# Attention by pairs of heads: transposes of both heads side by side, value tiles by pairs in one bank, weights' low parts on GpSimd

## The chip, the cores and the metric

One core of a Trainium2 chip runs the whole kernel. The metric is the device time of one execution in microseconds (us). The engines, by their names in the profile: PE is TensorE (matmuls, transposes), DVE VectorE, ACT ScalarE, POOL GpSimd, SP SyncE, which issues most DMA transfers. Each engine works through its own queue in order.

## The reference

One layer of a streaming encoder on a sequence of 1024 tokens with 1024 features.

```python
h = rmsnorm(x, norm_mix_g)
u, q, k, v = split(h @ w_in)            # u: 512 columns, q, k, v: 512 each (8 heads of 64)
y_pool = pool_mixer(u, pool_w, pool_b, pool_scale)   # 4 groups of 128 columns: trailing mean over
                                                     # 2/4/8/16 tokens minus the token, a 128x128 map
y_attn = chunk_attention(q, k, v, rel_bias)          # chunks of 64 tokens: own chunk and 8 before it,
                                                     # bias by clipped distance, softmax
x = x + concat(y_pool, y_attn) @ w_out
x = x + (gelu(conv3(h2 @ w_gate)) * (h2 @ w_up)) @ w_down   # h2 = rmsnorm(x), 2816 hidden columns
x = x + gate(x) * (p @ w_ple)                               # a gated input embedding of 256 columns
out = rmsnorm(x)
```

## The kernel before, in words

**Arithmetic.** Matrices are split into two parts of reduced precision (fp32r): a high part, which ScalarE makes by a rounding copy, and a low part, which VectorE makes by subtracting the high part from the source. `split` (L122, L123) does both. A product is three matmuls: high by high, high by low, low by high (`mm3`, L117 to L119). Wherever the text says "low part", it means that subtraction.

**Stages.** First x is loaded and split, and the first q/k block and half of V are projected (to about 54 us). Then comes the attention stage (54 to 280 us), then the output projection with the pooling mixer between its pieces (to 338 us), then the gated MLP and the embedding.

**The attention stage** goes through 28 units: four pairs of heads, and for each the token tiles (0, 1), 2, 3, 4, 5, 6, 7, of 128 tokens each. `unit(u)` does the following in TensorE's order.
- `probs_t` (L407) transposes the previous unit's probabilities into PSUM, banks 2 and 3 (chunk halves), what doesn't fit there into banks 6 and 7 (the far part). `probs_out` queues their evacuation: ScalarE's high part (L426) and VectorE's low part (L427) into PT, one buffer per head.
- `scores` (L383) multiplies q and k of this unit. `softmax` queues the minimum (L351), the exponential (L363), the reciprocal (L365) and the scaling (L361).
- Then TensorE gets some steps of `fill`, the generator over all projections that remain: q/k of pair 1 and 2, the second half of V, q/k of pair 3, and u in the order of the groups 2, 3, 0, 1. They use banks 0 and 1 in turn. A q/k half is evacuated at L263, a V tile at L254 and L255 with `v_outs`, a u half at L560.
- For an odd last tile, `values` (L451, L452) multiplies the transposed probabilities of two tiles by V, into a free one of banks 0 and 1.
- `run_later` emits up to eight steps of the window sums for u's groups 2 and 3 on GpSimd (`pool_out`, L575 to L589).

**The order of ScalarE's and VectorE's queues.** Every piece of such work is handed to `push` with a time within the unit, in us. `flush` sorts what has been pushed by these times and emits it. `now` is the unit's running time, which grows by 0.68 with each fill step, and `at` is the place within the current bank's projection. If a bank is needed whose evacuation is still unsorted (`owed`), `flush` comes early.

**Weights.** The blocks of w_in are loaded in turn into two raw buffers by SP (L171), and `split_later` queues their two high and two low parts (L475, L472). The weights of V's second half come between them by `v_weights`. The list `blocks_` holds the order of the blocks, with None for V. When block 1 is projected, the weights of V's second half are loaded once more and their first half is split once more; no matmul reads that. The raw buffer of this split is the one into which SP then loads blocks 4 and 5 of w_out (`rawo`).

**The output projection.** `out_weights` loads a block of w_out (L611) and splits it (L122, L123). `out_mm(d, h, bank, ...)` multiplies four blocks by the attention's output, 12 matmuls. `mix(g)` splits a group's pooled values (128x1024), multiplies them by its 128x128 map (six matmuls) and splits the result. TensorE's order in this stage is the program's: eight `out_mm` (z = 0 to 7) with mix(2), mix(3), mix(0), mix(1) between them, then the phase that adds the pooled part.

```python
raw = [f(4 * s, 1024) for s in range(2)]
rawo = [f(2 * s, 512) for s in range(4)]
```

Of the kernel before, what the change touches and what calls it, by code (L numbers as in the profile page):

```python
# [82 lines left out]
def trunk(tc, xT, pT, vecs, w_qk0, w_in, w_v, bias, counts, pool_w, w_out, w_up, w_down,  # L83
# [4 lines left out]
    with tc.tile_pool(name="sb", bufs=1) as sb, \  # L88
# [32 lines left out]
        def split(src, hi, lo, pinned=False):  # L121
            both = (act.activation(hi, src, AF.Copy),  # L122
                    dve.tensor_tensor(lo, src, rv(hi), ALU.subtract))  # L123
            if pinned:
                for i in both:
# [202 lines left out]


        for s in range(2):  # L330
            dve.memset(rv(PT[s][:, :, 0, P:2 * P]), 0.0)
            dve.memset(rv(PT[s][:, :, 5, 0:P]), 0.0)

        def load_bias(h):
            b = biasb[h % 3]
# [5 lines left out]
                pool.memset(b[64:128, 0:64], BIG)  # L341
            return turned

        def softmax(todo):

            for i, (x, b, ps, S, s_) in enumerate(todo):
                z = 2 * i / len(todo)

                def least(b=b, ps=ps, S=S, s_=s_):
                    if len(ps.shape) == 3:  # L350
                        dve.tensor_tensor_reduce(  # L351
                            S.rearrange("p (a b) -> p a b", a=2), ps,
                            b.rearrange("p (a b) -> p a b", a=2), 1.0, BIG, ALU.add, ALU.min, s_[:, 0:1])
                    else:
                        dve.tensor_tensor_reduce(S, ps, b, 1.0, BIG, ALU.add, ALU.min, s_[:, 0:1])

# [8 lines left out]
                push(2.95 + 0.55 * z, lambda s_=s_: dve.reciprocal(s_[:, 2:3], s_[:, 1:2]))  # L365
# [27 lines left out]
        def probs_t(u):  # L393

            c, ts = UNITS[u]
            total = key_tiles(u)

            def place(x, m):
                n = total * x + m
                return (2, HD * n) if n < 8 else (6, 384 + HD * (n - 8))  # L400

            todo = []
            for x in range(2):
                for m in range(total):
                    bank, col = place(x, m)
                    for y in range(2):
                        pe.transpose(PS[:, bank + y, col:col + HD], Sb[x][halves[y], m * P:(m + 1) * P],  # L407
                                     ident[halves[y], halves[y]], tile_position=(HD * y, 0))
                m = 0
                for t in ts:  # L410
                    nk = min(t + 1, BANDT)
                    i0 = max(0, t - 4) - (t // 2 * 2 - 4)
                    edge = min(nk, max(0, 8 - total * x - m))
                    parts = [p for p in ((0, edge), (edge, nk)) if p[1] > p[0]]
                    for a, b in parts:
                        bank, col = place(x, m + a)
                        todo.append((x, t % 2 * P, i0 + a, i0 + b, bank, PS[:, bank:bank + 2, col:col + HD * (b - a)]))
                    m += nk
            return todo

        def probs_out(todo):
            n = 0
            for x, q, a, b, bank, ps in todo:
                src = ps.rearrange("p a (k q) -> p a k q", q=HD)
                hi, lo = [PT[x][:, y, a:b, q:q + P].rearrange("p k (a q) -> p a k q", a=2) for y in range(2)]
                push(3.6 if bank > 3 else 0.3 * n, lambda hi=hi, src=src: act.activation(hi, src, AF.Copy))  # L426
                push(4.4 if bank > 3 else 3.55 + 0.05 * n if n else 2.6, lambda lo=lo, src=src, hi=hi: dve.tensor_tensor(lo, src, rv(hi), ALU.subtract))  # L427
                n += bank < 4

        credit, turns = 0.0, []  # L430

        def values(u):
            nonlocal credit
            c_, ts = UNITS[u]
            w = ts[-1] // 2
            if ts[-1] % 2 == 0:
                return
            while c_ >= 2 and len(v_ready) < 2 * w + 2 or u < NU - 1 and at[0] < 1.6:
                next(fill)
                credit -= 1  # L440
                now[0] += STEP
            flush()
            ks = list(range(max(0, 2 * w - 4), 2 * w + 2))
            bank = (bankn[0] + 1) % 2 if u < NU - 1 else 5
            Os = [PS[:, bank, 256 * j:256 * j + 256] for j in range(2)]
            for j in range(2):
                pt = PT[j]
                O = Os[j]
                for n_, k in enumerate(ks):
                    idx = k - (2 * w - 4)  # L450
                    pe.matmul(O, V[:, k, 2 * c_ + j], pt[:, 0, idx], start=n_ == 0, stop=False)  # L451
                    pe.matmul(O, V[:, k, 2 * c_ + j], pt[:, 1, idx], start=False, stop=n_ == len(ks) - 1)  # L452
# [14 lines left out]
        def split_later(ct, parts, soon=False):  # L467

            t = now[0] - 0.3 if soon else max(5.2, now[0] + 0.4)
            for i, (src, hi, lo) in enumerate(parts):  # L470
                def low(src=src, hi=hi, lo=lo, end=i == len(parts) - 1):
                    dve.tensor_tensor(lo, src, rv(hi), ALU.subtract)  # L472
                    if end:
                        there.add(ct)
                push(t + 0.7 * i * (not soon), lambda src=src, hi=hi: act.activation(hi, src, AF.Copy))  # L475
                push(t + (0.25 + 0.02 * i if soon else 0.8 + 0.7 * i), low)
# [41 lines left out]
        def project_v():  # L518
            v_weights(1)
            flush()  # L520
            order = [(t, z) for t in range(NTOK) for z in range(2)]
            order[1:3] = order[2:0:-1]
            order[-3:-1] = order[-2:-4:-1]
            banks = {}
            for t, z in order:
                if z == 0:
                    bankn[0] += 1
                    banks[t] = bankn[0] % 2
                    if banks[t] in owed:
                        flush()  # L530
                ps = PS[:, banks[t], 0:256]
                paired = t in (0, 1, NTOK - 2, NTOK - 1)
                if (t, z) == (NTOK - 2, 1):
                    weights(8 + 3)
                for k in range(4 * z, 4 * z + 4):
                    mm3(ps, XTH[t // 4][:, k, t % 4 * P:(t % 4 + 1) * P],
                        XTL[t // 4][:, k, t % 4 * P:(t % 4 + 1) * P], wv2[z][0][:, k % 4], wv2[z][1][:, k % 4],
                        k == 0, k == KT - 1)
                    if k % 2:
                        at[0] = 0.36 * (k + 1) if not paired else 0.36 * (k - 3) if z and t % 2 else 0.0  # L540
                        yield True
                if z:
                    hi, lo = v_outs(t, 1, ps)
# [110 lines left out]
        def unit(u):  # L654
# [3 lines left out]
            if u < NU:  # L658
                c, ts = UNITS[u]
                for h in range(2 if ts[-1] > 3 else 1):  # L660
                    while not all((c, x, h) in laid for x in range(2)):
                        next(fill)
                        lay_due(u - 1)
                        flush()
            if u:
                probs_out(probs_t(u - 1))
            if u < NU:
                softmax(scores(u))
# [776 lines left out]
```

## Time and profile before

| | us |
|---|---|
| median of 3 runs | 1140.84 (1140.73 to 1143.66) |
| the profiled execution | 1138.46 |
| its span | 1136.7 |
| TensorE busy in it | 1116.6 (98%) |
| VectorE busy | 866.1 (76%) |
| ScalarE busy | 589.0 (52%) |
| GpSimd busy | 144.2 (13%) |

All times in the text are on the clock of this profiled execution, from the start of its span, which is 1.76 us shorter than the execution. A line of a group of instructions gives the line of the kernel, engine, operation, what it writes and reads, the shape and the count; then busy us and the mean ns of one; then the idle time of the engine ahead of it and what ended that. A line of the timeline begins with its start and its length, for xN from the first start to the last end. A line of a window gives its length, then for PE, weight loads, DVE, ACT and POOL the busy us and the instructions, then the granted clock, the DMA share and GB/s.

### The profile page before, as it was taken

To read this page: it belongs to the slowest core of one execution; us is meant where nothing else is said; L and a number is where in the kernel's file an instruction comes from. 1 tells how busy PE (TensorE), PEld (TensorE's weight loads), DVE (VectorE), ACT (ScalarE), POOL (GpSimd) and SP (SyncE) were. 2 spreads that over 40 slices of the span, in tenths; PEclk is the share of its full clock that TensorE was granted. 3 is DMA by queue.
4 is the path that set the end of the run, shared out by engine and by line. 5 is a ranking of instruction groups with operands and counts; after the bars stand their busy time and mean duration, and the time that the engine had idled before them with its cause. 6 is when DMAs were issued, how large, how long until landed. Compare 5 with 4: busy or idle time off the path is not lost.

```text
span 1136.7 us, 16213 instructions
## 1 busy us (share of the span) xinstructions
PE 1116.6 (98%) x5914; PEld 934.5 (82%) x5914; DVE 866.1 (76%) x1508; ACT 589.0 (52%) x1052; POOL 144.2 (13%) x188
## 2 busy tenths in 40 slices
PE   9999998999999999999999999999999999999997
PEld 7988886888788888888888888888888888888887
DVE  8577757688757888887787777878888789986845
ACT  8376667665654554444444444444444445574634
POOL 0000000064002210120112110211030102000000
PEclk9999999999999999999999999999999999999999
DMA  8111120115500154575557655765576555520003
GB/s 280 36 37 43 38 61 1 59 38 174 178 12 17 42 155 147 134 170 151 133 151 161 159 139 150 155 162 144 149 162 163 139 148 124 155 93 19 1 31 118
DMA packets 64879, 125.91 MB, mean 111 GB/s; under 512 B 7328, under 2 KB 8736, under 8 KB 64800
## 3 DMA queue, kind: packets, MB, share of 16 engines
q1 hardware_dynamic: 50688, 99.38, 26.9%
q0 software_dynamic: 13824, 25.17, 13.8%
q8 instruction: 46, 0.75, 0.3%
q10 hardware_dynamic: 288, 0.33, 0.1%
q14 instruction: 33, 0.27, 0.1%
HBM read 110.18 MB, written 14.68 MB: 110 GB/s over the span
## 4 chain that ended last, share of the span: by engine, by line
PE 92%; DVE 3%; ACT 2%; issue 2%; DMA 1%; SPq 0%; POOL 0%; POOLq 0%; DVEq 0%; ACTq 0%
PE PS L117 29%; PE PS L118 28%; PE PS L119 28%; PE PS L383 2%; PE PS L452 2%; PE PS L451 2%; PE PS L407 2%; DVE F L351 1%; ACT R L122 1%; DMA F<-in_w_qk 1%; DVE B L427 0%; ACT F L602 0%; PE PS L751 0%; DVE F L361 0%; DMA F<-in_w_out 0%
## 5 line engine op out<-in xcount | busy, mean ns | idle before, releaser
L117 PE MATMUL PS<-R 128*128 128x512 f32 (+1 forms) x1104 | 425.0, 385 | 3.4 <-DVE F L263 1.7
L118 PE MATMUL PS<-R 128*128 128x512 f32 (+1 forms) x1104 | 421.6, 382 | 0.1
L119 PE MATMUL PS<-R 128*128 128x512 f32 (+1 forms) x1104 | 421.4, 382 | 0.0
L117 PEld LDWEIGHTS PS<-R 128*128 128x128 f32 x1104 | 207.5, 188 | 47.7 <-issue 2.1
L118 PEld LDWEIGHTS PS<-R 128*128 128x128 f32 x1104 | 207.6, 188 | 40.2 <-DVE R L228 1.3
L119 PEld LDWEIGHTS PS<-R 128*128 128x128 f32 x1104 | 207.5, 188 | 40.3
L122 ACT ACTIVATE R<-F 128x512 fp32r<-128x512 f32 (+2 forms) x221 | 138.3, 637 | 176.9 <-PE PS L118 80.7
L123 DVE TENSOR_TENSOR R<-F,R 128x512 fp32r<-128x512 f32 (+2 forms) x221 | 153.1, 704 | 41.0 <-ACT R L122 39.1
L1144 DVE TENSOR_TENSOR F<-F,PS 128x512 f32<-128x512 f32 x140 | 92.6, 681 | 6.5 <-PE PS L119 6.2
L834 DVE TENSOR_TENSOR F<-F 128x512 f32<-128x512 f32 x88 | 60.5, 687 | 45.6 <-DMA F<-in_w_up 44.9
L122 ACT ACTIVATE BQ<-RW 128x512 fp32r<-128x512 f32 x90 | 52.6, 622 | 78.3 <-PE PS L118 74.2
L1087 POOL DMA_DIRECT2D RW<-Yd x56 | 49.5, 884 | 261.9 <-DMA RW<-Yd 199.9
L1087 POOL DMA_DIRECT2D RW<-in_w_down x40 | 35.7, 937 | 230.8 <-DMA RW<-in_w_down 193.2
L123 DVE TENSOR_TENSOR BQ<-RW,BQ 128x512 fp32r<-128x512 f32 x90 | 59.0, 684 | 2.8 <-PE PS L118 2.1
L118 PE MATMUL PS<-BQ 128*128 128x512 f32 x140 | 54.6, 390 | 0.1
L119 PE MATMUL PS<-BQ 128*128 128x512 f32 x140 | 54.5, 389 | 0.0
L117 PE MATMUL PS<-R,BQ 128*128 128x512 f32 x140 | 54.5, 389 | 0.0
L118 PE MATMUL PS<-R,BQ 128*128 128x512 f32 x140 | 54.5, 389 | 0.0
L119 PE MATMUL PS<-R,BQ 128*128 128x512 f32 x140 | 54.5, 389 | 0.0
L117 PE MATMUL PS<-BQ 128*128 128x512 f32 x140 | 54.5, 389 | 0.0
L970 ACT ACTIVATE F<-F,vec 128x1024 f32<-128x1024 f32 (+1 forms) x25 | 28.6, 1143 | 46.8 <-DVE F L945 42.0
L363 ACT ACTIVATE F<-F,small 128x640 f32<-128x640 f32 (+4 forms) x64 | 44.0, 690 | 13.2 <-DVE small L351 11.5
(179 smaller groups left out, 1706.4 us busy)
## 6 DMA issues: line engine op xcount, KB each, us to landing
F<-in_w_up SPq DMA_DIRECT2D x91, 256.0 KB, 3.9
RW<-Yd SPq DMA_DIRECT2D x60, 256.0 KB, 3.7
RW<-Yd POOLq DMA_DIRECT2D x56, 256.0 KB, 4.9
RW<-in_w_down SPq DMA_DIRECT2D x50, 256.0 KB, 2.9
RW<-in_w_down POOLq DMA_DIRECT2D x40, 256.0 KB, 6.1
Yd<-F SPq DMA_DIRECT2D x40, 256.0 KB, 3.4
F<-in_w_in SPq DMA_DIRECT2D x10, 512.0 KB, 3.4
F<-in_xT SPq DMA_DIRECT2D x16, 256.0 KB, 6.1
```

The source lines that it names most:

```text
L117: pe.matmul(ps, ahi, bhi, start=first, stop=False, skip_group_check=more)
L118: pe.matmul(ps, ahi, blo, start=False, stop=False, skip_group_check=more)
L119: pe.matmul(ps, alo, bhi, start=False, stop=last, skip_group_check=more)
L122: both = (act.activation(hi, src, AF.Copy), dve.tensor_tensor(lo, src, rv(hi), ALU.subtract))
L123: dve.tensor_tensor(lo, src, rv(hi), ALU.subtract))
L363: push(1.9 + 0.85 * z, lambda S=S, s_=s_: act.activation(S, S, AF.Exp, bias=s_[:, 0:1], scale=-1.0, accum_out=s_[:, 1:2]))
L383: pe.matmul(PS[:, places[x][y], 0:wide], q[halves[x], t * P:(t + 1) * P], k[halves[x], ki + y * wide:ki + (y + 1) * wide], start=i == 0, s ...
L407: pe.transpose(PS[:, bank + y, col:col + HD], Sb[x][halves[y], m * P:(m + 1) * P], ident[halves[y], halves[y]], tile_position=(HD * y, 0))
L834: return dve.tensor_tensor(rawu[to], rawu[a], rawu[b], op)
L970: act.activation(y, Gb[:, 2 + a:2 + b], AF.Identity, bias=vec[:, C_CB + fi:C_CB + fi + 1], scale=cw(2))
L1087: pool.dma_start(t, src, accum_op=ALU.add)
L1144: dve.tensor_tensor(t, t, PS[:, 4 + d], ALU.subtract if n in (1, 5) else ALU.add)
```

## The change

It touches five places. (1) PT holds one buffer per precision instead of one per head, and both heads' transposes of a key tile stand side by side, so that one evacuation takes both heads: for a unit with five key tiles two pieces (1024 and 256 elements) instead of three. (2) The evacuations' and the softmax's push times are other ones, which depend on whether values follow (`valued`). (3) The second half of V is projected by pairs of tiles, both in one bank, and its evacuation is queued for the pair; q/k and u halves are evacuated at 3.6 or later. (4) The low parts in `split_later` go to GpSimd, but for block 9 and those that are wanted soon. (5) Each mix stands one `out_mm` earlier.

```diff
-        PT = [r(136 + 12 * s, 3072).rearrange("p (x k q) -> p x k q", x=2, k=6) for s in range(2)]
+        PT = [r(136 + 12 * y, 3072).rearrange("p (k x q) -> p k x q", x=2, k=6) for y in range(2)]
...
-                push(2.95 + 0.55 * z, lambda s_=s_: dve.reciprocal(s_[:, 2:3], s_[:, 1:2]))
-                push(3.9 + 0.1 * z if x else 3.0 + 0.55 * z, scaled)
+                push(max(2.95 + 0.01 * z, 1.91 + 0.85 * z) if valued else 2.95 + 0.55 * z, lambda s_=s_: dve.reciprocal(s_[:, 2:3], s_[:, 1:2]))
+                push(3.9 + 0.1 * z if x else 3.0 + (0.01 if valued else 0.55) * z, scaled)
...
             def place(x, m):
-                n = total * x + m
+                n = 2 * m + x
                 return (2, HD * n) if n < 8 else (6, 384 + HD * (n - 8))
...
-        def probs_out(todo):
-            n = 0
-            for x, q, a, b, bank, ps in todo:
-                src = ps.rearrange("p a (k q) -> p a k q", q=HD)
-                hi, lo = [PT[x][:, y, a:b, q:q + P].rearrange("p k (a q) -> p a k q", a=2) for y in range(2)]
-                push(3.6 if bank > 3 else 0.3 * n, lambda hi=hi, src=src: act.activation(hi, src, AF.Copy))
-                push(4.4 if bank > 3 else 3.55 + 0.05 * n if n else 2.6, lambda lo=lo, src=src, hi=hi: dve.tensor_tensor(lo, src, rv(hi), ALU.subtract))
-                n += bank < 4
+        def probs_out(todo, valued):
+            for q, a, b, bank, ps in todo:
+                src = ps.rearrange("p a (n q) -> p n a q", q=HD)
+                hi, lo = [pt[:, a:b, :, q:q + P].rearrange("p k x (a q) -> p (k x) a q", a=2) for pt in PT]
+                far = bank > 3
+                push(3.5 if far else 0.0, lambda hi=hi, src=src: act.activation(hi, src, AF.Copy))
+                push((3.55 if valued else 4.4) if far else 2.5 if valued else 3.7,
+                     lambda lo=lo, src=src, hi=hi: dve.tensor_tensor(lo, src, rv(hi), ALU.subtract))
...
-                    dve.tensor_tensor(lo, src, rv(hi), ALU.subtract)
+                    (dve if soon or ct == 8 + 1 else pool).tensor_tensor(lo, src, rv(hi), ALU.subtract)
...
-            order = [(t, z) for t in range(NTOK) for z in range(2)]
-            order[1:3] = order[2:0:-1]
-            order[-3:-1] = order[-2:-4:-1]
+            for t0 in range(0, NTOK, 2):
+                bankn[0] += 1
+                bank = bankn[0] % 2
+                if bank in owed:
+                    flush()
+                order = [(t, z) for t in (t0, t0 + 1) for z in range(2)]
+                if t0 in (0, NTOK - 2):
+                    order[1:3] = order[2:0:-1]
+                for i, (t, z) in enumerate(order):
+                    ps = PS[:, bank, 256 * (t % 2):256 * (t % 2) + 256]
...
+                            at[0] = 1.44 * i + 0.36 * (k % 4 + 1)
+                            yield True
+                for z in range(2):
+                    t = t0 + z
+                    hi, lo = v_outs(t, 1, PS[:, bank, 256 * z:256 * z + 256])
                     push(now[0], hi)
                     push(now[0] + 0.5, lo)
-                    owed.add(banks[t])
                     v_ready.append(t)
+                owed.add(bank)
...
-                    push(now[0], lambda: qk_out(x, h, ps))
+                    push(max(now[0], 3.6), lambda: qk_out(x, h, ps))
...
-                push(now[0] + 0.2, lambda: dve.tensor_tensor(U[:, g, HIST + h * 512:HIST + (h + 1) * 512], ps,
+                push(max(now[0], 3.6), lambda: dve.tensor_tensor(U[:, g, HIST + h * 512:HIST + (h + 1) * 512], ps,
...
-            if 2 <= z <= 5:
-                mix((2, 3, 0, 1)[z - 2])
+            if 1 <= z <= 4:
+                mix((2, 3, 0, 1)[z - 1])
```

Lines shift with the edit: L472 is L469 after it, L427 L426, L575 L571, L589 L585, L611 L607.

In GpSimd's queue, the low parts of block 1 now stand where the window sums of u's group 2 end and those of group 3 begin (F is the work area, R and B are split data). The rows before:

```order
L575 TENSOR_TENSOR F<-F 128x265
L585 TENSOR_TENSOR F<-F,small 128x8
L588 TENSOR_TENSOR F<-F,small 128x248
L586 TENSOR_TENSOR F<-F 128x8
L589 TENSOR_TENSOR F<-F 128x248
L575 TENSOR_TENSOR F<-F 128x271
L575 TENSOR_TENSOR F<-F 128x269
```

And after the change:

```order
L571 TENSOR_TENSOR F<-F 128x265
L581 TENSOR_TENSOR F<-F,small 128x8
L584 TENSOR_TENSOR F<-F,small 128x248
L582 TENSOR_TENSOR F<-F 128x8
L585 TENSOR_TENSOR F<-F 128x248
L469 TENSOR_TENSOR B<-F,B 128x512
L571 TENSOR_TENSOR F<-F 128x271
L469 TENSOR_TENSOR B<-F,B 128x512
L571 TENSOR_TENSOR F<-F 128x269
```

Two subtractions have come in, at L469; those of block 0 stand in the same way among the first sums of group 2. The end of the same queue's part in the attention stage, after the change, is the last window sum with the two low parts of the V half that nothing reads:

```order
L571 TENSOR_TENSOR F<-F 128x257
L581 TENSOR_TENSOR F<-F,small 128x16
L584 TENSOR_TENSOR F<-F,small 128x240
L582 TENSOR_TENSOR F<-F 128x16
L585 TENSOR_TENSOR F<-F 128x240
L469 TENSOR_TENSOR R<-F,R 128x512 x2
```

The two subtractions (x2) stood in VectorE's queue before, and GpSimd's ended with the last window sum. In SyncE's queue, the loads of V's half and of w_out stand in the same order as before, with the semaphores on which each waits. Before:

```order
L171 DMA F<-in_w_v 128x1024 [waits DMAHW7_49,DMAHW3_49,DVE_49]
L171 DMA F<-in_w_v 128x1024 [waits DMAHW6_49,DMAHW0_49,DVE_49]
L611 DMA F<-in_w_out 128x512 [waits DMAHW0_49]
L611 DMA F<-in_w_out 128x512
L773 DMA F<-in_xT 128x1024 [waits PE_49,Activation_49,Pool_49]
L773 DMA F<-in_xT 128x1024 [waits DMAHW4_49,PE_49]
L611 DMA F<-in_w_out 128x512 [waits DMAHW7_49,DMAHW5_49,DVE_49]
L611 DMA F<-in_w_out 128x512 [waits DVE_49]
```

And after:

```order
L171 DMA F<-in_w_v 128x1024 [waits DMAHW7_49,DMAHW3_49,Pool_49]
L171 DMA F<-in_w_v 128x1024 [waits DMAHW6_49,DMAHW0_49,Pool_49]
L607 DMA F<-in_w_out 128x512 [waits DMAHW0_49]
L607 DMA F<-in_w_out 128x512
L770 DMA F<-in_xT 128x1024 [waits PE_49,Activation_49]
L770 DMA F<-in_xT 128x1024 [waits DMAHW4_49,PE_49]
L607 DMA F<-in_w_out 128x512 [waits DMAHW7_49,DMAHW5_49,Pool_49]
L607 DMA F<-in_w_out 128x512 [waits Pool_49]
```

The loads have kept their places; four of the waits on VectorE are waits on GpSimd now. The third and fourth load of w_out are its blocks 4 and 5.

More of the change, by code (lines that the diff above doesn't have):

```diff
@@ L330, in trunk @@
         for s in range(2):
-            dve.memset(rv(PT[s][:, :, 0, P:2 * P]), 0.0)
-            dve.memset(rv(PT[s][:, :, 5, 0:P]), 0.0)
+            dve.memset(rv(PT[s][:, 0, :, P:2 * P]), 0.0)
+            dve.memset(rv(PT[s][:, 5, :, 0:P]), 0.0)
         def load_bias(h):
@@ L342, in load_bias, with softmax @@
             return turned
-        def softmax(todo):
+        def softmax(todo, valued):
             for i, (x, b, ps, S, s_) in enumerate(todo):
@@ L398, in place @@
             def place(x, m):
-                n = total * x + m
+                n = 2 * m + x
                 return (2, HD * n) if n < 8 else (6, 384 + HD * (n - 8))
-            todo = []
             for x in range(2):
@@ L408, in probs_t @@
                                      ident[halves[y], halves[y]], tile_position=(HD * y, 0))
[L409 to L418, printed above, removed]
-            return todo
-        def probs_out(todo):
-            n = 0
-            for x, q, a, b, bank, ps in todo:
-                src = ps.rearrange("p a (k q) -> p a k q", q=HD)
-                hi, lo = [PT[x][:, y, a:b, q:q + P].rearrange("p k (a q) -> p a k q", a=2) for y in range(2)]
-                push(3.6 if bank > 3 else 0.3 * n, lambda hi=hi, src=src: act.activation(hi, src, AF.Copy))
-                push(4.4 if bank > 3 else 3.55 + 0.05 * n if n else 2.6, lambda lo=lo, src=src, hi=hi: dve.tensor_tensor(lo, src, rv(hi), ALU.subtract))
-                n += bank < 4
+            todo, m = [], 0
+            for t in ts:
+                nk = min(t + 1, BANDT)
+                i0 = max(0, t - 4) - (t // 2 * 2 - 4)
+                for a, b in ((0, min(nk, 4)), (4, nk)):
+                    if b > a:
+                        bank, col = place(0, m + a)
+                        todo.append((t % 2 * P, i0 + a, i0 + b, bank, PS[:, bank:bank + 2, col:col + 2 * HD * (b - a)]))
+                m += nk
+            return todo
+        def probs_out(todo, valued):
[6 more added lines that the diff above has]
+                     lambda lo=lo, src=src, hi=hi: dve.tensor_tensor(lo, src, rv(hi), ALU.subtract))
         credit, turns = 0.0, []
@@ L446, in values @@
             for j in range(2):
-                pt = PT[j]
                 O = Os[j]
@@ L450, in values @@
                     idx = k - (2 * w - 4)
-                    pe.matmul(O, V[:, k, 2 * c_ + j], pt[:, 0, idx], start=n_ == 0, stop=False)
-                    pe.matmul(O, V[:, k, 2 * c_ + j], pt[:, 1, idx], start=False, stop=n_ == len(ks) - 1)
+                    pe.matmul(O, V[:, k, 2 * c_ + j], PT[0][:, idx, j], start=n_ == 0, stop=False)
+                    pe.matmul(O, V[:, k, 2 * c_ + j], PT[1][:, idx, j], start=False, stop=n_ == len(ks) - 1)
             for j in range(2):
@@ L520, in project_v @@
             flush()
-            order = [(t, z) for t in range(NTOK) for z in range(2)]
-            order[1:3] = order[2:0:-1]
-            order[-3:-1] = order[-2:-4:-1]
[L524 to L543, printed above, removed]
+            for t0 in range(0, NTOK, 2):
[8 more added lines that the diff above has]
+                    ps = PS[:, bank, 256 * (t % 2):256 * (t % 2) + 256]
+                    if (t0, i) == (NTOK - 2, 2):
+                        weights(8 + 3)
+                    for k in range(4 * z, 4 * z + 4):
+                        mm3(ps, XTH[t // 4][:, k, t % 4 * P:(t % 4 + 1) * P],
+                            XTL[t // 4][:, k, t % 4 * P:(t % 4 + 1) * P], wv2[z][0][:, k % 4], wv2[z][1][:, k % 4],
+                            i == 0 and k == 0, k == KT - 1, True)
+                        if k % 2:
+                            at[0] = 1.44 * i + 0.36 * (k % 4 + 1)
[3 more added lines that the diff above has]
+                    hi, lo = v_outs(t, 1, PS[:, bank, 256 * z:256 * z + 256])
@@ L664, in unit @@
                         flush()
+            valued = u > 0 and UNITS[u - 1][1][-1] % 2 == 1
             if u:
-                probs_out(probs_t(u - 1))
+                probs_out(probs_t(u - 1), valued)
             if u < NU:
-                softmax(scores(u))
+                softmax(scores(u), valued)
                 if u % PER == PER - 1:
```

## The prediction

> **What bounds the kernel now.** I read the page first: how busy each engine is, and which engine carries the chain that ended last.
>
> ```profile
> PE 1116.6 (98%) x5914; PEld 934.5 (82%) x5914; DVE 866.1 (76%) x1508; ACT 589.0 (52%) x1052; POOL 144.2 (13%) x188
> PE 92%; DVE 3%; ACT 2%; issue 2%; DMA 1%; SPq 0%; POOL 0%; POOLq 0%; DVEq 0%; ACTq 0%
> ```
>
> TensorE is the bound. The change takes no matmul away, so it can gain only what TensorE waits for, and lose by new waits. Work taken off VectorE and ScalarE counts only there. Next I read what ends TensorE's waits in the stretch where the second half of V is projected (127 to 181 us), and TensorE's busy time there.
>
> ```profile
> PE PS L407 <- DVE B L427: 2.0, 2, 1.8
> PE PS L452 <- DVE B L427: 2.0, 1, 2.0
> PE PS L117 <- DVE F L263: 1.7, 1, 1.7
> PE PS L117 <- DVE R L255: 1.2, 1, 1.2
> PE PS L451 <- ACT B L426: 0.8, 1, 0.8
> 127.00:137.00 10.00, 8.19 (x96) 7.48 (x97) 6.92 (x16) 6.08 (x13) 0.00 (x0) 1.00 0.17 52
> 147.00:157.00 10.00, 9.79 (x116) 9.24 (x117) 7.93 (x24) 9.02 (x23) 0.29 (x2) 1.00 0.24 68
> 157.00:167.00 10.00, 8.81 (x65) 8.23 (x64) 5.96 (x16) 5.04 (x12) 0.00 (x0) 1.00 0.19 54
> 167.00:180.00 13.00, 8.42 (x88) 6.92 (x88) 7.38 (x24) 9.31 (x23) 0.29 (x2) 1.00 0.12 40
> ```
>
> The waits add up to 7.7 us, and the idle time of the four windows to 1.81 + 0.21 + 1.19 + 4.58 = 7.8. All of them are late evacuations: of transposed probabilities (L426/L427), a V bank (L255), a q/k bank (L263). The change rearranges these.
>
> The second place is what surrounds the last projection and the output projection: GpSimd, the loads of w_out, and VectorE's queue behind them.
>
> ```profile
> 240.00:250.00 10.00, 10.00 (x70) 8.10 (x69) 8.51 (x22) 7.56 (x16) 9.06 (x16) 1.00 0.16 52
> 250.00:260.00 10.00, 9.70 (x85) 8.22 (x85) 8.66 (x18) 5.22 (x12) 9.26 (x13) 1.00 0.32 105
> 260.00:270.00 10.00, 10.00 (x73) 8.78 (x69) 5.82 (x10) 4.80 (x10) 9.37 (x15) 1.00 0.54 160
> 269.72 1.15 POOL L589 TENSOR_TENSOR F<-F 128x240 f32<-128x240 f32 x1
> 264.11 0.88 DVE L472 TENSOR_TENSOR R<-F,R 128x512 fp32r<-128x512 f32 x1 [0.79 <-ACT R L475]
> 265.02 5.01 SPq L611 DMA_DIRECT2D F<-in_w_out  x3
> F<-in_w_out SPq DMA_DIRECT2D x16, 256.0 KB, 2.8
> 267.92 1.67 ACT L122 ACTIVATE R<-F 128x512 fp32r<-128x512 f32 x3 [1.12 <-DMA F<-in_w_out]
> 268.59 4.63 DVE L123 TENSOR_TENSOR R<-F,R 128x512 fp32r<-128x512 f32 x6 [0.91 <-ACT R L122]
> 302.11 1.23 DVE L123 TENSOR_TENSOR B<-F,B 128x1024 fp32r<-128x1024 f32 x1 [0.17 <-ACT B L122]
> 268.50:280.00 11.50, 11.50 (x58) 9.72 (x57) 10.85 (x15) 6.28 (x11) 2.37 (x4) 1.00 0.69 239
> 280.00:303.40 23.40, 21.03 (x93) 16.87 (x91) 22.18 (x46) 16.92 (x28) 0.00 (x0) 1.00 0.59 179
> 303.39 0.50 PE L118 MATMUL PS<-B 128*128 128x512 f32 x1 [0.77 <-DVE B L123]
> 305.33 0.39 PE L118 MATMUL PS<-R 128*128 128x512 f32 x1
> 310.36 0.39 PE L119 MATMUL PS<-R 128*128 128x512 f32 x1
> ```
>
> Column five of the windows is GpSimd: with its window sums it is busy 27.7 of the 30 us from 240 to 270, and done at 270.87. SyncE issues the load of w_out's block 4 at 265.02, right behind the first half (264.11) of a second split of V's first weights, which nothing reads but whose raw buffer the load takes over. The block lands after 2.8, ScalarE rounds it, and its low part is the first of the row at 268.59. From there VectorE is busy 10.85 + 22.18 = 33.0 of 34.8 us until the low part of mix(1) ends at 303.34 and releases the matmul at 303.39. So the mixes wait for a VectorE queue that starts with block 4. After that two out_mm (24 matmuls, 305.00 to 310.36 and one interval of (310.36 - 305.33)/22 = 0.229) lead to the pooled phase at 310.59.
>
> **The change part by part.** *Pairs of V tiles in one bank, transposes side by side, the new push times.* Prices of the evacuations, from the groups by form of 127 to 181 us:
>
> ```profile
> L427 DVE TENSOR_TENSOR B<-PS,B 128x640 fp32r<-128x640 f32 x4 | 3.3, 818 | 0.0
> L427 DVE TENSOR_TENSOR B<-PS,B 128x384 fp32r<-128x384 f32 x6 | 3.3, 543 | 0.0
> L427 DVE TENSOR_TENSOR B<-PS,B 128x256 fp32r<-128x256 f32 x6 | 2.5, 411 | 0.0
> L255 DVE SCALAR_TENSOR_TENSOR R<-PS,small,R 128x256 fp32r<-128x256 f32 x8 | 3.9, 482 | 4.6 <-ACT R L254 4.6
> L254 ACT ACTIVATE R<-PS,small 128x256 fp32r<-128x256 f32 x8 | 3.7, 464 | 2.7 <-PE PS L119 2.7
> ```
>
> The low parts of a full unit cost VectorE 818 + 543 + 411 = 1.77 us in three pieces. By their slope, (818 - 411)/384 = 1.06 ns an element, the new two (1024 and 256 elements) cost 1.23 + 0.41 = 1.64. What matters is where they stand: ahead of values, the near low part now follows the softmax's first scaling and both follow no V low part. The 32 pieces fewer on each engine are otherwise worth nothing, since TensorE seldom waits for either elsewhere.
> - V and q/k banks (1.2 + 1.7): a bank is now filled by two tiles before the next is needed, twice the time for an evacuation. I take both waits as gone; but four evacuations then come at once (2 x 0.464 and 2 x 0.482), and following the new rows through those units leaves about 0.6 before one set of values.
> - Transposes (2.0): they wait until the preceding near piece is out of its banks. I leave 0.7, where a V pair stands ahead of it.
> - Values (2.0 + 0.8): the far low part now comes right behind the near one. I leave 0.5.
>
> So 7.8 - 1.8 = 6.0: **-6.0 us**. Ends: all gone, -7.8; a pair's evacuation falling just where a low part fell, -3. No row shows a read from PSUM that alternates between two banks every 64 elements. Below nothing has no reason, since the elements are the same. At most a quarter more (411 for 256 elements by L427 against 482 by L255), 0.3 us on the near piece, lies within that end.
>
> Where no values follow, the near low part stands behind all scaling (3.7). It is one piece of up to 1024, so ScalarE's high part, ahead of it, ends later by 384 elements, about 0.4 us by the same slope. Two late units have few projection steps to cover that: 2 x 0.4 = **+0.8**, between 0 and 1.5.
>
> *The low parts on GpSimd.* Of eighteen lows, those of blocks 5, 10, 6, 7, 2, 3 and of V's first half find GpSimd idle (its first window sum starts at 234.39) and are read a projection later. At twice their time they cost nothing. If a projection began sooner, it would wait about 1.3 us.
>
> ```profile
> 234.39 2.19 POOL L575 TENSOR_TENSOR F<-F 128x271 f32<-128x271 f32 x3 [23.79 <-DVE small L365]
> L899 POOL TENSOR_TENSOR F<-TB x4: 1284/1294/1737, 340.4 to 376.7; 128x512 f32<-128x512 f32 x4
> L909 POOL TENSOR_TENSOR TB<-TB 128x512 f32<-128x512 f32 x4 | 8.0, 1996 | 28.9 <-DVE TB L903 18.9 <-DVE R L123 10.0
> 250.25 3.99 POOL L575 TENSOR_TENSOR F<-F 128x271 f32<-128x271 f32 x4
> 250.15 1.74 DVE L472 TENSOR_TENSOR B<-F,B 128x512 fp32r<-128x512 f32 x2
> 261.00 2.16 POOL L575 TENSOR_TENSOR F<-F 128x269 f32<-128x269 f32 x3
> ```
>
> The other six stand among and behind the window sums: two of block 0, two of block 1, then both of the V half that nothing reads. GpSimd is full there, so what is put in shifts its end. A GpSimd operation on 128x512 takes 1.29 (L899). Up to the first unread low there are five: 270.87 + 5 x 1.29 = 277.3. Block 0's low also waits for its high part (its raw data came at least that late before: up to +1.7). Against that, VectorE's L472 pairs no longer slow the sums: four operations took 3.99 beside such a pair where three took 2.16 later, 1.1 us a pair, two pairs, 2.3 in all. So 276.7. **SyncE now waits for GpSimd there**, and every load of w_out behind block 4 waits in SyncE's queue: 276.7 instead of 265.02, +11.7. The way from the issue to the low part (landing 2.8 and rounding, 268.59 - 265.02 = 3.6) is as before, so block 4's low part starts about 280.3 instead of 268.59: **+11.7**.
>
> VectorE's queue is in order, so u's evacuations and mix(2) and mix(3) lie behind that row. Three 512 lows (2.49 us for four of them, so 0.6 each) now stand behind mix(1): -1.8. Of the queue's idle time, 34.8 - 33.0 = 1.7, I let all go. *One out_mm fewer between the mixes:* behind mix(1) stand three instead of two, 12 more matmuls of 0.229: +2.7. The sum is 11.7 - 1.8 - 1.7 + 2.7 = **+10.9** for the start of the pooled phase. The 3.1 us that TensorE waits in the mixes before (300.15 to 304.43) is inside it, since the chain runs over VectorE. Ends: +8.5, if GpSimd gains another 2.3 from a quieter VectorE; +14, if each of the five lows takes L909's 2.0 instead of 1.29.
>
> ```profile
> 302.13 0.49 PE L117 MATMUL PS<-B 128*128 128x512 f32 x1 [1.60 <-ACT B L122]
> ```
>
> Sum: -6.0 + 0.8 + 10.9 = **+5.7 us**. The profiled execution took 1138.46 (span 1136.7 and 1.76 around it), so 1144.2; the median of the runs is 2.4 above it, so **1146.5 us**. 0.3% (3.4 us) is about what a measurement of this kernel can tell from no change.
>
> **The rivals.**
> 1. *GpSimd is done in time (faster).* Without VectorE's lows its sums run at 0.65 (261.00: 2.16 for three) instead of about 1.0, and the unread low ends by 265. Then the w_out chain starts no later than before: -6.0 + 0.8 - 1.8 - 1.7 + 2.7 = -6.0, about 1135. The point from which it decides is 271: a low that ends there makes the output term as large as the V term's gain. Against it: 27.7 of 30 us busy, with five more of 1.29. Chance 0.12.
> 2. *The two cancel.* Block 4 is late by 7 only, so the output term is 10.9 - 4.7 = +6.2, and all of the V waits go (-7.8): with the +0.8 that is -0.8, about 1140. For it: both are ends that I hold possible. Chance 0.20.
> 3. *GpSimd and VectorE hold each other up.* The row at 250.25 shows that a sum of 0.65 takes up to 1.1 beside VectorE's subtraction, and that the pair of subtractions takes 1.74 instead of 1.38. If each of the five lows waits for one such subtraction (0.69), it takes 2.0 as L909's do, block 4 is 3.5 later still: +9.2, 1150. The Trainium skill, page "SBUF — State Buffer", section "SBUF: two separate sides", has it as a rule: a GpSimd operation and a VectorE operation with two SBUF inputs share a port pair that whoever starts first keeps for the whole instruction, and the other blocks. The trace agrees in that row. Chance 0.18.
> 4. *Pairs don't do what they say.* The V waits only move to the values: -2 instead of -6, +9.7, 1150.5. For it: VectorE has 5.96 to 7.93 us of work in 10 there, so a late evacuation is an order, not a load. Chance 0.08.
>
> **How the numbers follow.** My forecast has 0.42; with rivals 3 and 4 slower has 0.68, same 0.20, faster 0.12. The range takes rival 2 with some 2 us below it, and above my sum at its bad ends, -3 + 1.5 + 13 = +11.5: 1138 to 1152.5.
>
> **What would show it.** After the change SyncE's load of w_out's block 4 waits for GpSimd and goes out right behind its first subtraction after the last window sum; VectorE stands idle ahead of block 4's low part; TensorE has new gaps in the first out_mm's block 4 to 7 and ahead of mix(2) and mix(1). The gaps of the V stretch shrink from 7.8 to about 2. I am wrong if GpSimd's last window sum ends no later against TensorE, or if that load does not wait for it, or if TensorE finds other matmuls for the time.

## The result and the profile after

The changed kernel takes 1139.83 us (median of 12 runs, 1138.78 to 1142.72), the kernel before in the same runs 1140.49 (1137.27 to 1143.66): a ratio of the means of 1.0002, interval 0.9990 to 1.0014. Forecast were 1146.5 and slower. The time lies in the range, but there is no difference that can be measured: of the cases it came out as the second rival, in which gain and loss cancel, though not by that rival's terms (see below).

The page of the changed kernel, its engines and its chain:

```profile
PE 1120.2 (98%) x5914; PEld 936.5 (82%) x5914; DVE 848.5 (74%) x1456; ACT 587.2 (51%) x1020; POOL 165.3 (14%) x208
PE 84%; DVE 5%; issue 4%; POOL 3%; DMA 2%; ACT 1%; POOLq 0%; DVEq 0%; ACTq 0%
```

VectorE has 18 us less to do and GpSimd 21 more, and GpSimd, which was not on the chain, now holds 3% of it. TensorE's waits in the whole kernel, the longest groups:

```profile
PE PS L117 <- ACT F L598: 2.3, 2, 1.6
PE PS L117 <- ACT F L918: 2.0, 2, 1.4
PE PS L117 <- ACT B L122: 1.9, 1, 1.9
PE PS L119 <- DVE R L123: 1.7, 1, 1.7
PE PS L406 <- DVE B L426: 1.6, 3, 0.9
```

Nothing of the V stretch is left at the top. Its windows show the same (third field: TensorE's busy us; the stretch is shorter now and ends at about 175):

```profile
127.00:137.00 10.00, 9.86 (x116) 9.17 (x115) 6.93 (x15) 6.57 (x12) 0.00 (x0) 1.00 0.15 54
147.00:157.00 10.00, 10.00 (x103) 9.73 (x103) 7.83 (x27) 9.26 (x24) 0.29 (x2) 1.00 0.24 67
157.00:167.00 10.00, 9.64 (x97) 9.00 (x96) 5.39 (x15) 6.08 (x14) 0.00 (x0) 1.00 0.05 6
167.00:175.00 8.00, 7.68 (x71) 6.27 (x68) 5.34 (x13) 6.85 (x14) 2.20 (x4) 1.00 0.16 61
```

Of the 7.8 us of idle time there, 1.2 are left with the window from 137 (0.35, not shown). The first matmul of the output projection, in the timeline of before:

```profile
279.97 0.39 PE L117 MATMUL PS<-R 128*128 128x512 f32 x1
```

and in that of the changed kernel, with the first of the pooled phase (before: 310.59):

```profile
274.22 0.39 PE L117 MATMUL PS<-R 128*128 128x512 f32 x1
...
312.96 0.39 PE L117 MATMUL PS<-R 128*128 128x512 f32 x1
```

So up to the output projection 5.75 us are won, and within it 38.74 - 30.62 = 8.1 are lost. How, the timelines of GpSimd, SyncE, VectorE and TensorE after the change show:

```profile
266.19 0.70 POOL L585 TENSOR_TENSOR F<-F 128x240 f32<-128x240 f32 x1
266.85 2.53 POOL L469 TENSOR_TENSOR R<-F,R 128x512 fp32r<-128x512 f32 x2
268.16 5.18 SPq L607 DMA_DIRECT2D F<-in_w_out  x4
271.48 3.70 DVE L123 TENSOR_TENSOR R<-F,R 128x512 fp32r<-128x512 f32 x6 [10.15 <-ACT R L122]
277.33 0.50 PE L119 MATMUL PS<-R 128*128 128x512 f32 x1 [1.67 <-DVE R L123]
300.64 1.22 DVE L123 TENSOR_TENSOR B<-F,B 128x1024 fp32r<-128x1024 f32 x1
301.92 0.69 PE L118 MATMUL PS<-B 128*128 128x512 f32 x1 [0.76 <-DVE B L123]
```

The chain is the one forecast: the last window sum, the first unread low part (266.85 to about 268.1), block 4's load at 268.16, VectorE idle for 10.15 us and then full until mix(1)'s low part ends at 301.86. Block 4's low part starts 2.74 us ahead of the output projection, before it was 11.38 ahead: 8.6 us later, where 11.7 were forecast.

One more thing stands in the windows, in the column behind GpSimd's, the granted clock of TensorE:

```profile
278.10:281.50 3.40, 3.40 (x10) 2.62 (x9) 3.37 (x5) 1.15 (x2) 0.00 (x0) 0.51 0.87 277
302.00:305.40 3.40, 3.40 (x9) 2.64 (x9) 1.67 (x3) 2.72 (x5) 0.00 (x0) 0.51 0.83 272
```

Twice TensorE ran at half its clock for 3.4 us, so that its matmuls there took 1.7 us longer each time. The chain that ended last runs over VectorE beside the first of these stretches and over TensorE through the second, so by this profile only the second lengthened the stage. The profiled execution of before has none until 1130 us.

### The profile page after: what moved, and what is told of

Read it like the earlier page. It is cut to its first block, busy times and chain, and to the rows that moved or that the text cites. A ratio compares the mean times of both kernels' runs of the same rounds, so it can differ in the third digit from the quotient of the medians.

```text
span 1140.7 us, 16154 instructions
## 1 busy us (share of the span) xinstructions
PE 1120.2 (98%) x5914; PEld 936.5 (82%) x5914; DVE 848.5 (74%) x1456; ACT 587.2 (51%) x1020; POOL 165.3 (14%) x208
## 4 chain that ended last, share of the span: by engine, by line
PE 84%; DVE 5%; issue 4%; POOL 3%; DMA 2%; ACT 1%; POOLq 0%; DVEq 0%; ACTq 0%
PE PS L117 26%; PE PS L118 26%; PE PS L119 26%; POOL F L571 2%; PE PS L383 1%; DVE R L123 1%; PE PS L406 1%; PE PS L448 1%; PE PS L449 1%; DMA F<-in_w_up 1%; DMA F<-in_w_out 1%; DVE B L123 0%; POOL F L584 0%; DVE B L426 0%; POOL F L585 0%
## 5 line engine op out<-in xcount | busy, mean ns | idle before, releaser
L1084 POOL DMA_DIRECT2D RW<-Yd x56 | 49.2, 879 | 267.4 <-DMA RW<-Yd 201.6
```

Source lines behind the costliest of these rows:

```text
L1084: pool.dma_start(t, src, accum_op=ALU.add)
```

## The experiments

Times are medians, ratios are to the kernel before on the same chip, with their intervals. Where the text gives the start of the pooled phase, it is read from that run's trace.

**Without the unread half of V** (1). The second load and half split, which no matmul reads, are left out of the changed kernel.

```diff
-                    if (h, k) == (0, 2):
+                    if (h, k) == (0, 2) and ct != blocks_[-1]:
                         weights(behind)
```

> The changed kernel without the second load and half split of V's weights, which nothing reads. Theory A (the load of w_out's block 4 waits for GpSimd's unread low part at the end of its queue, and VectorE's queue and the mixes wait for that block): the load goes out before 262 us, VectorE's queue from block 4 to mix(1)'s low part ends by 294 instead of 301.9, the pooled phase starts about 7 us earlier than in the changed kernel, 1132 to 1134 us. Theory B (the loss comes from the mixes' new place and VectorE's queue itself, not from the load): 1138 to 1140 us, as the changed kernel.

1136.01 us, 0.9954 (0.9941 to 0.9967). By the ratios that is 5.5 us less than the changed kernel, where 6 to 8 were expected. Block 4 is loaded long before 262, but mix(2) still starts late, as ScalarE's timeline shows:

```profile
270.66 1.06 ACT L122 ACTIVATE B<-F 128x1024 fp32r<-128x1024 f32 x1 [9.36 <-POOL F L585]
```

It waits for GpSimd's last window sum, which I had left out, and the pooled phase starts at 309.05, 3.9 us earlier than in the changed kernel, where 7 were expected. The mixes have two conditions, w_out's block 4 and the sums themselves, and GpSimd's queue sets both.

**All low parts on VectorE** (2).

```diff
-                    (dve if soon or ct == 8 + 1 else pool).tensor_tensor(lo, src, rv(hi), ALU.subtract)
+                    dve.tensor_tensor(lo, src, rv(hi), ALU.subtract)
```

> The changed kernel with all low parts of split_later back on VectorE. Theory A: block 4 goes out right behind VectorE's unread low part, about 259 us, the attention stage keeps its gain of 5.8 us, so 1134 to 1136 us. Theory B: the queue and the mixes' place are as in the changed kernel, so 1138 to 1140 us.

1134.48 us, 0.9941 (0.9929 to 0.9953): theory A. The pooled phase starts at 303.88 instead of 312.96.

**The kernel before without the unread half** (3), by the same edit as in (1).

> The kernel before without the second load and half split of V's weights, which nothing reads. Theory A: block 4 is loaded some us earlier, the mixes' waits (3.1 us) go in part: 1137 to 1139 us. Theory B: no change, 1140 us.

1140.58 us, 0.9993 (0.9985 to 1.0002): no gain that can be measured. Block 4 was not what held the mixes as long as VectorE did the low parts; theory A was too generous here.

**The kernel before with the low parts on GpSimd** (4), the edit of (2) the other way round.

> The kernel before with only the low parts moved to GpSimd as in the change. Theory A: block 4 waits for GpSimd's unread low part, about 9 us later than before, without any gain in the attention stage: the pooled phase starts 5 to 8 us later, 1146 to 1149 us. Theory B: within 1 us of before.

1147.46 us, 1.0053 (1.0041 to 1.0065). The timelines of GpSimd, SyncE and VectorE:

```profile
273.72 2.54 POOL L472 TENSOR_TENSOR R<-F,R 128x512 fp32r<-128x512 f32 x2
275.03 5.07 SPq L611 DMA_DIRECT2D F<-in_w_out  x4
278.21 4.30 DVE L123 TENSOR_TENSOR R<-F,R 128x512 fp32r<-128x512 f32 x7 [10.66 <-ACT R L122]
```

The load goes out 10.0 us later than before (265.02), and the time follows by 6.0. In this trace the pooled phase starts at 320.01, 9.4 us later than before, above the 5 to 8 expected; three stretches of 3.41 us at half the clock lie ahead of it, in the trace of before there is none. Taken with (2), the sum closes within the intervals: everything but the low parts is worth 0.9941 - 1 = -6.7 us, the low parts alone +6.0, and both together were measured as +0.2.

**Only the pairs of V tiles** (5): the kernel before with the change's `project_v`.

> The kernel before with only the change's V projection (two tiles in one bank). Theory C (V pairs and the transposes' new order each take away part of the 7.8 us of waits between 127 and 181 us): the waits for V's and the q/k bank (2.9 us) go, those of transposes and values stay, 1137 to 1138.5 us. Theory D (one of the two parts does it all): 1134 to 1136 us, or no change.

1135.23 us, 0.9949 (0.9937 to 0.9961): theory D's first case. The V stretch has two waits left:

```profile
PE PS L452 <- DVE B L427: 1.8, 1, 1.8
PE PS L451 <- DVE R L255: 0.4, 1, 0.4
```

The waits for transposes (2.0) are gone too, though the transposes were as before. This trace doesn't show that the pairs took them away: TensorE ran at half its clock from 168.4 to 171.8, which gives the evacuations beside and behind it 1.7 us more. Its output projection starts at 275.59, 4.4 us earlier than before, with that stretch inside.

**Only the transposes side by side and the new push times** (6): the changed kernel with the old `project_v`, the low parts on VectorE and the mixes at their old place.

> The kernel before with only the transposes side by side and the new times in the queue (places 1 and 2, and the q/k and u evacuations at 3.6). Theory C: the waits of transposes and values (4.8 us) go in part, 1136.5 to 1138.5 us. Theory D: 1134 to 1136 us, or no change.

1145.31 us, 1.0038 (1.0022 to 1.0053), slower; neither theory had that. The waits in the V stretch:

```profile
PE PS L406 <- DVE B L426: 2.8, 2, 2.2
PE PS L117 <- DVE F L263: 2.4, 1, 2.4
PE PS L449 <- DVE B L426: 1.6, 1, 1.6
PE PS L448 <- ACT B L424: 0.8, 1, 0.8
PE PS L117 <- DVE R L255: 0.7, 2, 0.3
```

They add up to 8.3 instead of 7.7. The wait for a q/k bank is longer (L263: 2.4 instead of 1.7), which fits its evacuation put off to 3.6 with one tile in a bank, and so are the waits for transposes (2.8 instead of 2.0), which fits the near low part as one piece. That is 0.6 us of the 4.3. The trace holds two more pieces: from 225 us to the output projection TensorE is idle for 1.8 us instead of 0.8, and from 306.5 it runs at half its clock for 3.41 us. The runs went from 1142.3, the profiled one, to 1148.5, and what makes the rest was not settled.

**The mixes at their old place** (7): as (2), with each mix one out_mm later.

```diff
-            if 1 <= z <= 4:
-                mix((2, 3, 0, 1)[z - 1])
+            if 2 <= z <= 5:
+                mix((2, 3, 0, 1)[z - 2])
```

> The changed kernel with the low parts on VectorE and each mix one out_mm later, as before the change. Theory E (the mixes' chain ends no earlier for standing earlier, and the third out_mm behind mix(1) is the price): the 2.4 us that TensorE waits in the mixes go, 1131.5 to 1133.5 us. Rival (the earlier mixes are a gain of their own): 1135 to 1137 us.

1133.83 us, 0.9939 (0.9927 to 0.9951). The place of the mixes is worth nothing that can be measured beside (2): mix(1)'s low part ends 4 us later (298.4 instead of 294.4) with one out_mm fewer behind it, and the pooled phase starts at 305.7 instead of 303.9; the medians don't show that. The time lies between the two theories, and the waits did not go: TensorE waits 2.8 us in the mixes, 2.0 in (2). The ratio against (5) shows what the transposes and their times add once V goes by pairs: 1.4 us in the medians, within both intervals.

**The waits filled with matmuls** (8): 24 further matmuls, whose results nothing reads, in the changed kernel.

```diff
+        fill_up(8, 7)
         for z, d in enumerate(first_d):
             out_mm(d, 0, first_b[z], attn, True, False)
             if 1 <= z <= 4:
+                if z in (2, 4):
+                    fill_up({2: 7, 4: 9}[z], 1)
                 mix((2, 3, 0, 1)[z - 1])
```

> The changed kernel with 24 further matmuls whose results nothing reads, 8 ahead of the first out_mm, 7 ahead of mix(3), 9 ahead of mix(1), where TensorE waits anyway. Theory F (a window of 3.41 us in which TensorE works little is followed by 3.41 us at half its clock, 1.7 us each time): no such stretch between 270 and 310 us, the granted clock there is 1.00, and 1137 to 1138.5 us although there is more work. Rival (the clock falls for another reason): 1139.5 to 1141 us.

1142.20 us, 1.0011 (1.0003 to 1.0020), a miss, and no clean one: the scheduler places ScalarE's work anew behind the added matmuls, and mix(3) now waits longer for mix(2)'s evacuation. The waits, and TensorE's window behind them:

```profile
PE PS L117 <- ACT F L598: 3.4, 1, 3.4
...
290.00:295.00 5.00, 3.49 (x8) 2.84 (x9) 4.96 (x12) 4.84 (x8) 0.00 (x0) 0.52 0.65 197
```

Behind the filled places ahead of the first out_mm and of mix(1) the clock stays at 1.00. The new wait, ahead of mix(3), which the seven matmuls there don't fill, has 6.83 us at half the clock behind it, from 290.2 on. That speaks for theory F, but it tells nothing of the price.

**Only the twelve early low parts on GpSimd** (9): blocks 0 and 1 and the unread half (the second split of a block that is `in there` already) go back to VectorE.

```diff
-                    (dve if soon or ct == 8 + 1 else pool).tensor_tensor(lo, src, rv(hi), ALU.subtract)
+                    (dve if soon or ct in (8 + 1, 0, 1) or ct in there else pool).tensor_tensor(lo, src, rv(hi), ALU.subtract)
```

> The changed kernel with the low parts of blocks 0 and 1 and of the unread half of V on VectorE, the other twelve on GpSimd. Theory A (the twelve early low parts cost nothing on GpSimd, the six late ones cost it all): as with all of them on VectorE, 1133.5 to 1135.5 us. Rival (each low part on GpSimd costs a share of the 6 us): 1137 to 1139 us.

1132.80 us, 0.9932 (0.9915 to 0.9948), the fastest kernel of the study, 0.7 us below theory A's range and by the ratios 8 us below the changed one. The early ones cost nothing; whether they gain against (2) stays within the intervals. Mix(2) starts in time:

```profile
265.86 1.06 ACT L122 ACTIVATE B<-F 128x1024 fp32r<-128x1024 f32 x1 [1.91 <-POOL F L585]
```

**Only the unread half back on VectorE** (10): the same edit without `0, 1`.

> The changed kernel with only the two low parts of the unread half of V on VectorE. Theory A, as the run without that half refined it (what blocks 0 and 1 put into GpSimd's queue still delays the window sums, and mix(2) waits for the last of them, but block 4 no longer does): 1135 to 1137 us, block 4 loaded by 260 us. Rival (blocks 0 and 1 alone make the loss): 1139 to 1140 us.

1137.38 us, 0.9974 (0.9963 to 0.9985), as refined behind (1), at the upper end. Block 4 is loaded at 260.28 and ready; mix(2) is not:

```profile
263.50 6.00 DVE L123 TENSOR_TENSOR R<-F,R 128x512 fp32r<-128x512 f32 x6 [0.61 <-ACT R L122]
270.82 1.06 ACT L122 ACTIVATE B<-F 128x1024 fp32r<-128x1024 f32 x1 [6.31 <-POOL F L585]
```

Four low parts in GpSimd's queue put off the last sum from 265.8 to 270.8 (5.2 us by four times 1.29), and VectorE's subtractions of w_out, six in 6.00 us instead of 3.70 alone, meet the sums still to be done. By the ratios blocks 0 and 1 cost 4.8 us ((10) against (9)) and the unread half 3.2 (the changed kernel against (10)).

**The parts that paid, together** (11): as (7), without the unread half.

> The changed kernel with the low parts on VectorE, each mix one out_mm later, and without the unread half of V: the parts that paid, together. If block 4's way is what holds the mixes, TensorE's last waits there (3 us) go in part: 1131 to 1133 us. If the window sums hold them, 1133.5 to 1134.5 us, as without that.

1134.99 us, 0.9949 (0.9934 to 0.9964): the window sums hold the mixes; ScalarE waits 6.3 us for the last of them before it splits mix(2). Without the unread half, VectorE's subtractions of w_out start at 258.5 and run beside the last sums, which end at 267.4 instead of 265.8 in (7). Leaving out work that nothing reads gained nothing here.

**Matmuls of one column** (12): 48 of them ahead of the first out_mm of (9), with no engine to wait for.

```diff
+        for _ in range(48):
+            pe.matmul(PS[:, 7, 0:1], ident, ones, start=True, stop=True)
```

> The run with twelve early low parts on GpSimd, with 48 further matmuls of one column (about 0.11 us each, 5.4 us) ahead of the first out_mm, whose results nothing reads; the order of ScalarE's and VectorE's work behind them shifts with that, so its time is not compared, only the granted clock. Theory F (the clock halves behind a window of 3.41 us in which TensorE streams little, whatever it waits for): a stretch of 3.41 us at half the clock begins within 274 to 284 us, where that run had none. Rival (only waits for other engines do it, busy narrow matmuls don't): 1.00 there.

Theory F, by the windows:

```profile
270.00:275.00 5.00, 5.00 (x27) 4.22 (x25) 4.97 (x7) 2.02 (x4) 0.00 (x0) 1.00 0.87 283
280.00:285.00 5.00, 5.00 (x25) 5.00 (x25) 3.97 (x11) 1.35 (x3) 0.00 (x0) 0.50 0.68 218
285.00:290.00 5.00, 5.00 (x25) 5.00 (x25) 0.10 (x1) 0.00 (x0) 0.00 (x0) 0.50 0.20 52
```

By the profile TensorE is busy in every us and waits for nothing, yet at 279.5 the clock falls to half and stays there for 13.65 us, four times 3.41, until wide matmuls have run again. (The 48 show as 96, with up to 0.35 us each at the low clock, so this took longer than planned; its time, 1149.5 in one run, is not compared. They multiply plain fp32 data, the kernel's wide matmuls fp32r, and this run alone doesn't tell width from format.)

## Why the prediction was wrong, point by point

- *The V stretch, -6.0, and the late units, +0.8.* Forecast -5.2, measured -5.75 up to the output projection. Right in sum, wrong in its parts: I gave the V and q/k banks 2.9 us and the transposes and values 4.8. By the ratio of (5) the pairs of V tiles do it nearly alone; by (6) the rest alone is a loss. So the parts are not independent, and a row that names who is late doesn't name who made it late. Why the waits for transposes went was not settled: in the trace of before the longest of them ends at 179.61, and VectorE's last evacuation of V ahead of it starts at 165.18, so V's evacuations did not make that one late.
- *The low parts on GpSimd: the step that failed.* The mechanism was right: by (2), (4), (9) and (10) the whole loss comes from the six late low parts, by the load of block 4 and, which I had missed, by the window sums that the mixes themselves need. The size was wrong, 11.7 against 8.6. I had block 0's low part wait up to 1.7 us for its high part; it did not. And I gave GpSimd back 2.3 us for VectorE's absent subtractions; its sums took 32.2 instead of 36.5 us (229.12 to 266.89 less four low parts of 5.6 in all, against 234.39 to 270.87), so 4.3. These two make 3.7 us, and the way from the load to the low part was 0.25 shorter; against that, the five low parts took 6.9 us instead of 6.45, and the first sum stood 5.3 us earlier instead of 5.75. In (1) and (10), where block 4 came in time and VectorE did w_out's subtractions beside the sums, the same sums took 35.2 us. So about 3 of the 4.3 us came from the delay itself: while the load waited, VectorE had nothing to do that slows the sums. My term had left that out.
- *VectorE's queue and the mixes' place, -1.8 - 1.7 + 2.7 = -0.8.* From block 4's low part to the pooled phase it took 41.5 us instead of 42.0, of which 1.7 are the slow clock from 302.0 on: -2.2 without that. By (7) the earlier mixes are neither a gain nor a loss.
- *The sum.* With the measured terms, -5.75 + 8.6 - 2.2 = +0.7 us instead of +5.7: below what can be told from no change. The miss of 5.0 is 3.1 for GpSimd, 1.4 for the queue and 0.5 for the V stretch.
- *The base.* I set the profiled execution of before 2.4 us below the median and carried that over as a constant. It is not one. In 18 runs of the kernel before beside (5) to (8), the mean clock went from 0.998 (1138.43 us) to 0.993 (1143.03 us): the slow stretches differ from run to run. The pair of profiled executions alone would have said 1142.72 - 1138.46 = +4.3, near the forecast: 1.7 of it are the slow stretch on the chain, of which that of before had none, and 1.6 the longer rest of the program (see the end of this section). Such a pair must not be taken for the result.
- *Rival 1* (GpSimd done in time) fell. *Rival 2* (the two cancel) gave the outcome, but not by its terms: it had block 4 late by 7 and the V term with the late units at -7.0, measured were 8.6 and -5.75, and VectorE's queue made up for it. That the time lies in the range is in part luck. *Rival 3* (the two engines holding each other up) had the price of a low part too high: in the changed kernel three of the four among the sums took 1.29 and one 1.74. The row of (10) shows the effect on VectorE instead, 6.00 against 3.70. *Rival 4* fell with (5).

What stays open: from the start of the pooled phase on, the changed kernel's profile is 1.6 us longer than before's (827.7 against 826.1), with 2.0 us of waits on L918. In the other runs' profiles this rest of the program, which no edit touches, took between 824.8 and 828.1 us; I don't know what sets it.

## What to carry to other kernels

Before moving work to an idle engine, see which of its hours are idle: twelve operations were free on GpSimd while it had nothing else, and six beside and behind its own work cost all that the rest of the change won. Follow every consumer at the end of that engine's queue, a load that takes over a buffer as well as the results that were queued there before. And price a change from several executions where the clock varies; one profile without a slow stretch is a lucky base.

## What the runs showed of the hardware

The clock of TensorE halves for a multiple of 3.41 us behind a window in which it streams little. In the changed kernel the window ahead of the first slow stretch, and one that had none behind it:

```profile
274.70:278.10 3.40, 1.73 (x7) 0.97 (x6) 3.35 (x7) 2.79 (x5) 0.00 (x0) 1.00 0.81 277
288.40:291.80 3.40, 1.89 (x7) 1.28 (x8) 3.27 (x9) 3.40 (x7) 0.00 (x0) 1.00 0.75 199
```

TensorE need not stand still for the whole window: 1.73 us of 3.40 busy were too few here. By the busy time no sharp limit comes out, since a window of (10) with 1.63 (283.8 to 287.2) and one of (5) with 1.59 (294.7 to 298.1) had no slow stretch behind them. What was streamed separates them better. An estimate from all traces, between 40 and 1100 us: I count windows in steps of 3.41 us from a slow stretch, leave out those that run at half the clock themselves, and take 0.227 us for 512 columns, as in a steady row of matmuls. Behind each of the 12 windows of which the columns filled at most 0.39 the clock fell, and behind none that they filled to 0.40 or more. The narrow matmuls of (12) filled 0.004 of theirs. The Trainium skill, page "TensorE: Matmul & The Clock Gate", section "What's actually happening", has the clock fall after an idle window of about 3.4 us. The length agrees; that the window must be idle does not, by these rows, nor does waiting matter as such: in (12) TensorE was busy without a gap. So a wait of 2 us can cost 2 us or 3.7 (with the 1.7 of a slow stretch), depending on where the windows fall; that they fall differently from run to run fits the spread of the clock above, but was not shown by itself.

The page "SBUF — State Buffer" of the Trainium skill, section "SBUF: two separate sides", lets a GpSimd operation and a VectorE operation with two SBUF inputs block each other. The trace agrees: six subtractions took 3.70 us with GpSimd at rest and 6.00 beside its sums.
